# A trunk step on one core: a gate's product behind two lower halves, three norm sums one unit on, and two window sums behind the last split of an activation sum

## The chip, the cores and the metric

The kernel runs on one core of a Trainium2 chip. A core has a matrix engine (PE, with its weight loads shown as PEld), three elementwise engines (DVE, ACT, POOL) and a queue that issues most transfers (SP). The metric is the device time of one execution in microseconds (us), the median over the runs; lower is better.

## The reference

One inference step of a two-layer trunk on 1024 prompt tokens and 8 x 8 sample tokens, 1088 columns in all, all in float32. Layer 0 is a Mamba-2 (SSD) mixer, layer 1 a pooling mixer, each behind a modulated norm; a last norm follows. Cut to what this case touches:

```python
# layer 0, per group g of 8 (256 channels each)
y, new_ssm = ssd_scan(xs, dt, A, Bm, Cm, ssm_prev)
y = (y + d_skip[:, None] * xs).reshape(b, L, D_INNER)
gated = (y * silu(z)).reshape(b, L, N_GROUPS, D_INNER // N_GROUPS)
gated = gated * rsqrt(mean(gated * gated, -1) + EPS)          # one norm per group
out = (gated.reshape(b, L, D_INNER) * norm_g) @ w_out
# layer 1
uz = h @ w_in;  u, z = uz[..., :2048], uz[..., 2048:]
for g, w in enumerate((2, 4, 8, 16)):                          # 512 channels each
    win_sum = cs[off:off+L] - cs[off-w:off-w+L]                # sum over the last w rows of u
    groups.append(win_sum / cnt - u[g])
mixed = einsum(groups, w_group) * ch_scale * silu(z)
out = mixed @ w_out
```

## The kernel before

Activations lie with channels on the 128 partitions and the 1088 tokens along the row. Every float32 operand of a large product is split into an upper half `hi` (an ACT copy to the short type) and a lower half `lo` (on DVE: the value minus `hi`), and a product is three matmuls: hi by hi, hi by lo, lo by hi. A matmul chunk is 368, 368 and 352 columns (`CH`) in layer 0's direct products, and 272 columns in the products that save a multiplication by sums of blocks (tile name `st`).

The Python code writes instructions in program order, and the framework's scheduler then fixes one order for each engine; `self.tc.issue_after(ins)` around a call says that what is written inside is to be placed behind `ins` in that order. Each engine runs its own list strictly in turn, so an instruction that waits holds all that stand behind it. Semaphores make engines wait for one another.

Layer 0's scan is `scan_group(g, T)`, a generator for each of 8 groups. Its steps are small, so `ssd_layer` fills PE between them with units of other work from `self.fill` (`beside`): projections first, and from group 4's last steps on the units of the output product, `op_first` and then `op_unit` (one chunk, 12 matmuls on four pairs of halves). `FILL[g]` says how many units follow each scan step. When a group's steps are done, its tail goes on as `rest` in the loop of the next group: step `next(rest)` at `i == 0` runs the norm sum, and step `next(rest)` at `i == 3` scales the rows by it.

The tail of a group: `gate(q)` multiplies 128 channels of the rows by the gate (L748 on DVE, tile `xbc<-xbc,z`), and squares them (L749 on ACT). `zsum` adds the two squares (L791 on DVE). L763 on PE sums over the channels with a matrix of ones (tile `ms`); ACT takes logarithm and exponent; a row goes out to memory (L768 on SP, `rsd`) and comes back to all partitions (L771 on SP, `rs`). L775 on DVE scales the gated rows with it, and they are stored for the output product (L778).

For group 4 the second gate is not made in the tail itself: it is kept as `gate_late` and called in `proj_group`, behind the evictions of the last projection, at the place where the output product begins. There `op_part_load` prepares four pairs of halves: a row tile `gr` comes in, ACT makes `gh` (L805), and DVE makes the lower half `gl` (L806). `op_first` multiplies first with all the upper halves (L830, L831), then with the lower ones (L835), and only then evicts its three chunks (L847 on DVE).

For groups 4, 5 and 6 the sum of the squares is put behind the eviction of a filling unit (`self.zsum(ins)` in `ssd_layer`); where the unit returns no eviction, it is made with L763.

Layer 1 begins with `pool_layer`: `plain_pairs` makes two plain tiles of u and z, and beside them `act_sums` forms sums and differences of activation blocks (L1001 on DVE) and splits them into halves with `split` (ACT L1004, DVE L1005), into new tiles `t` and into the blocks `hh`, `hl`. `fast_pairs` then runs products of 272 columns. Their weights come as sums too: `w_sums` adds weight blocks on POOL (L1042 and L1043, tile `sw`; L1047, L1049), and `split_half` splits each (ACT L182, DVE L184, tile `w`). After the first pair of products, `u_pool` is called for the two plain tiles as well (p = 0 and 1): it forms running sums over w rows by doubling (L929 on DVE: the first reads `u` at step 1, the later ones `ws`).

Of the kernel before, what the change touches and what calls it, by code (L numbers as in the profile page):

```python
# [8 lines left out]
F32 = mybir.dt.float32  # L9
F32R = mybir.dt.float32r  # L10
AF = mybir.ActivationFunctionType
ALU = mybir.AluOpType
# [17 lines left out]
PLAIN = 2  # L30
# [69 lines left out]
class Build:  # L100
# [296 lines left out]
    def proj_group(self, G):  # L397

        raws = []
        for ii in range(4):  # L400
            w = self.stream_next()
            raw = self.proj_begin(G, ii)
            raws.append(raw)
            if (G["g"], ii) == (BESIDE[-1], 3):
                self.proj_end(G, 2, raws[2], True)
                ps = [self.mm_tile() for _ in CH]
                for k in range(8):
                    for c, j in ((0, k), (1, k), (2, 0), (2, k)) if k == 1 else ((0, k), (1, k), (2, k))[:3 if k else 2]:
                        self.mm1(ps[c], w, j, self.hn[j], CH[c], j == 0, j == 7)
                    for j in (0, 1) if k == 1 else (k,) if k else ():  # L410
                        self.slots.free(*self.hn[j])
                    if 0 < k < 4:
                        next(self.prep)
                    elif k in ():
                        self.load_x(0, k - 0)
                    if k < 7:
                        yield
                for c in range(3):
                    ins = self.proj_evict(G, ii, raw, ps[c], c, False)
                with self.tc.issue_after(ins.ins):  # L420
                    for _ in range(2):
                        next(self.prep)
                    with self.tc.issue_after(self.op_hi):
                        self.gate_late()
                yield
                self.late = lambda: self.proj_end(G, ii, raw, True)
                return
            ada = self.ada_do(self.ada_plan[G["g"], ii]) if (G["g"], ii) in self.ada_plan else iter(())
            for c in range(3):
                ps = self.mm_tile()  # L430
                self.mm3(ps, w, self.hn, CH[c])
                self.proj_evict(G, ii, raw, ps, c, (G["g"], ii) != (BESIDE[-1], 2))
                if c != (0, 0, 2, 0)[ii]:
                    next(ada, None)
                yield
# [366 lines left out]
    def op_split(self, raw, part):  # L802
        hi, lo = self.slots.get("gh", F32R, short=True), self.slots.get("gl", F32R, short=True)
        with self.tc.issue_after(self.front_copy) if 0 < part < 3 else contextlib.nullcontext():
            self.op_hi = self.nc.scalar.activation(hi, raw, AF.Copy).ins  # L805
        self.nc.vector.tensor_tensor(out=lo, in0=raw, in1=hi.bitcast(F32), op=ALU.subtract)  # L806
        self.slots.free(raw)
        return hi, lo

# [107 lines left out]
    def u_pool(self, p, U):  # L917

        nc, gi, (raw, rv) = self.nc, p // 4, U
        w = WINDOWS[gi]  # L920
        npl = self.gp2.tile([P, 9, 15], F32, tag="npl", bufs=2, name=self.name("npl"))
        nc.gpsimd.tensor_copy(npl[:, 0:1, :], raw[:, 1024:1039].unsqueeze(1))
        nc.gpsimd.tensor_copy(npl[:, 1:9, :], rv[:, :, 8:23])
        nc.sync.dma_start(self.io["npT"][p], npl)
        s, step, m = raw, 1, WIDE
        while step < w:
            d = self.slots.get("ws", wide=True)
            m -= step
            nc.vector.tensor_tensor(out=d[:, :m], in0=s[:, :m], in1=s[:, step:step + m], op=ALU.add)  # L929
            if step > 1:  # L930
                self.slots.free(s)
            s, step = d, 2 * step
        o = 16 - w
        nc.vector.tensor_tensor(out=s[:, o:o + w - 1], in0=s[:, o:o + w - 1], in1=self.kc[:, K_CNT + 15 * gi:K_CNT + 15 * gi + w - 1], op=ALU.mult)
        pl = self.slots.get("pl")
        nc.vector.scalar_tensor_tensor(out=pl[:, :NP], in0=s[:, o:o + NP], scalar=1.0 / w, in1=raw[:, 15:1039], op0=ALU.mult, op1=ALU.subtract)
        sv = s[:, 1039:1223].rearrange("p (b w) -> p b w", w=23)[:, :, o:o + 8]
        nc.vector.scalar_tensor_tensor(out=pl[:, NP:TOK].rearrange("p (b i) -> p b i", i=8), in0=sv, scalar=1.0 / w, in1=rv[:, :, 15:23],
                                       op0=ALU.mult, op1=ALU.subtract)
        self.slots.free(raw, s)  # L940
        nc.sync.dma_start(self.pld[p], pl)
        self.slots.free(pl)
# [50 lines left out]
    def act_sums(self):  # L993


        nc, sl, x = self.nc, self.slots, self.x
        h1, h2 = slice(0, HALF), slice(HALF, TOK)
        self.T = {}

        def sub(out, x, y):  # L1000
            nc.vector.tensor_tensor(out=out, in0=x, in1=y, op=ALU.subtract)  # L1001

        def split(x, hi, lo):
            nc.scalar.activation(hi, x, AF.Copy)  # L1004
            nc.vector.tensor_tensor(out=lo, in0=x, in1=hi.bitcast(F32), op=ALU.subtract)  # L1005

        def new(i, k, x):
            t = sl.get("t", F32R)
            self.T[i, k] = t
            split(x, t[:, h1], t[:, h2])  # L1010

        t1 = []
        for k in range(4):
            p, r = x[k], x[k + 4]
            t1.append(x[k - 1][:, h2] if k % 2 else p[:, h1])
            sub(t1[k], p[:, h2], p[:, h1])
            sub(p[:, h2], r[:, h2], p[:, h2])
            sub(r[:, h2], r[:, h2], t1[k])
            sub(r[:, h1], r[:, h1], r[:, h2])
            new(2, k, r[:, h2])  # L1020
            new(3, k, p[:, h2])
            yield
            new(4, k, r[:, h1])
            sl.free(r)
            if k % 2:
                sl.free(p)
            yield
        for k in range(4):
            p, q = self.hn[k]
            split(t1[k], p[:, h2], q[:, h2])  # L1030
        sl.free(x[0], x[2])
# [554 lines left out]
    def ssd_layer(self):  # L1586
        nc, sl = self.nc, self.slots
# [6 lines left out]
        for g in range(8):  # L1594
            sc = self.scan_group(g, T[g])
            for i, n in enumerate(FILL[g]):
                next(sc)
                for j in range(n):
                    ins = next(self.fill)
                    if ins:  # L1600
                        self.zsum(ins)
                    if i == 0 and j == 0:
                        next(rest, None)
                    elif i == 3 and j == 0:
                        with self.tc.issue_after(self.hins), self.tc.issue_after(ins.ins) if ins else contextlib.nullcontext():
                            next(rest, None)
# [350 lines left out]
```

## Time and profile before

| what | value |
|---|---|
| median of 3 runs | 1591.47 us (1590.93 to 1593.26) |
| profiled execution | 1587.95 us |
| its span, first to last instruction | 1586.1 us |
| mean granted clock of the matrix engine | 0.997 |
| PE / PEld busy | 1569.5 us (99%) / 1506.7 us (95%) |
| DVE / ACT / POOL busy | 1299.7 / 790.7 / 536.9 us |

Busy time is the time with at least one instruction of the engine under way. In a timeline a row gives start, length, engine, line, operation, tiles (out<-in), shape and count; in square brackets stands the idle time of the engine before it and what ended it. Consecutive matmuls overlap, so their pace is read from start to start. A row of the waits gives the waiting instruction, what it waited for, the total in us, how many times, and the longest. A row of the stretches gives the busy time of each engine (with counts), then the granted clock of PE, the share of the transfer engines' time and GB/s.

### The profile page before, as it was taken

How to read it: one execution, taken by the hardware profiler on the slowest of the kernel's cores; microseconds unless marked ns; L12 is line 12 of the kernel's file. 1: busy time of each engine (PE TensorE's matmuls, PEld its weight loads, DVE VectorE, ACT ScalarE, POOL GpSimd, SP SyncE). 2: the span in 40 equal slices, each digit the busy share in tenths (PEclk: the TensorE clock that was granted, in tenths of full speed). 3: DMA queues.
4: the chain of work that ended last, by engine and by line, in shares of the span. 5: the costliest groups of instructions: out<-in, count | busy, mean ns of one | idle time of the engine just before them, and what ended most of it. 6: DMA issues, size and time to landing. Idle time of an engine off the chain costs nothing.

```text
span 1586.1 us, 30716 instructions
## 1 busy us (share of the span) xinstructions
PE 1569.5 (99%) x11946; PEld 1506.7 (95%) x11946; DVE 1299.7 (82%) x2152; ACT 790.7 (50%) x1512; POOL 536.9 (34%) x558
## 2 busy tenths in 40 slices
PE   9999999999999999999999999999999999999997
PEld 7899999999999899989999999999999999999997
DVE  6974789888899889889888858998889777667886
ACT  6663344466766666665455437533332233233364
POOL 0133556522332414121211232776566630000241
PEclk9999999999999999999999999999999999999999
DMA  9422232355555555678999532233333379565783
GB/s 356 168 101 96 84 113 81 111 190 174 165 172 174 164 201 162 217 255 294 325 335 313 173 124 73 70 136 101 117 114 117 102 250 366 138 178 176 163 175 124
DMA packets 122304, 275.57 MB, mean 174 GB/s; under 512 B 18192, under 2 KB 59312, under 8 KB 122160
## 3 DMA queue, kind: packets, MB, share of 16 engines
q1 hardware_dynamic: 117840, 259.79, 48.0%
q0 software_dynamic: 4032, 12.72, 4.6%
q8 instruction: 94, 1.54, 0.4%
q10 hardware_dynamic: 288, 1.11, 0.2%
q14 instruction: 50, 0.41, 0.1%
HBM read 201.12 MB, written 70.23 MB: 171 GB/s over the span
## 4 chain that ended last, share of the span: by engine, by line
PE 88%; DVE 6%; ACT 2%; POOL 2%; issue 1%; DMA 1%; DVEq 0%; ACTq 0%; POOLq 0%
PE st L1079 11%; PE st L1077 11%; PE st L1078 11%; PE mm L190 11%; PE mm L191 11%; PE mm L192 10%; PE op L1297 2%; PE op L1298 2%; PE op L1296 2%; PE y L645 2%; PE S L623 2%; PE y L649 1%; PE tr L584 1%; PE am L261 1%; POOL sw L1042 1%; PE tr L581 1%
## 5 line engine op out<-in xcount | busy, mean ns | idle before, releaser
L1079 PE MATMUL st<-hh,w 128*128 128x272 f32 x832 | 240.6, 289 | 0.0
L1077 PE MATMUL st<-hh,w 128*128 128x272 f32 x832 | 240.4, 289 | 0.0
L1078 PE MATMUL st<-hl,w 128*128 128x272 f32 x832 | 240.4, 289 | 0.0
L1079 PE MATMUL st<-t,w 128*128 128x272 f32 x624 | 179.9, 288 | 0.6 <-DVE w L184 0.6
L1077 PE MATMUL st<-t,w 128*128 128x272 f32 x624 | 180.0, 288 | 0.0
L1078 PE MATMUL st<-t,w 128*128 128x272 f32 x624 | 179.5, 288 | 0.0
L190 PE MATMUL mm<-hh,wh 128*128 128x368 f32 (+1 forms) x528 | 179.2, 339 | 0.0
L191 PE MATMUL mm<-hl,wh 128*128 128x368 f32 (+1 forms) x528 | 174.3, 330 | 0.0
L192 PE MATMUL mm<-hh,wl 128*128 128x368 f32 (+1 forms) x528 | 173.4, 328 | 0.0
L1077 PEld LDWEIGHTS st<-hh,w 128*128 128x128 f32 x832 | 157.0, 189 | 0.0
L1078 PEld LDWEIGHTS st<-hl,w 128*128 128x128 f32 x832 | 157.0, 189 | 0.0
L1079 PEld LDWEIGHTS st<-hh,w 128*128 128x128 f32 x832 | 156.7, 188 | 0.0
L182 ACT ACTIVATE w<-wr 128x512 fp32r<-128x512 f32 x104 | 65.0, 629 | 165.7 <-PE st L1079 134.1
L631 POOL TENSOR_TENSOR hd<-h,cd 128x256 f32<-128x256 f32 x56 | 46.1, 824 | 291.4 <-DVE h L632 126.6
L1296 PE MATMUL op<-b,w 128*128 128x272 f32 x448 | 129.6, 289 | 0.0
L1297 PE MATMUL op<-b,w 128*128 128x272 f32 x448 | 129.0, 288 | 0.2 <-DVE b L1225 0.2
L1298 PE MATMUL op<-b,w 128*128 128x272 f32 x448 | 129.1, 288 | 0.0
L190 PE MATMUL mm<-gh,wh 128*128 128x368 f32 (+1 forms) x372 | 125.3, 338 | 0.0
L192 PE MATMUL mm<-gh,wl 128*128 128x368 f32 (+1 forms) x372 | 122.5, 329 | 0.0
L191 PE MATMUL mm<-gl,wh 128*128 128x368 f32 (+1 forms) x372 | 122.3, 329 | 0.2 <-DVE gl L806 0.2
L1079 PEld LDWEIGHTS st<-t,w 128*128 128x128 f32 x624 | 117.5, 188 | 0.8 <-DVE w L184 0.8
L1077 PEld LDWEIGHTS st<-t,w 128*128 128x128 f32 x624 | 117.8, 189 | 0.4 <-ACT w L182 0.3
(310 smaller groups left out, 4613.3 us busy)
## 6 DMA issues: line engine op xcount, KB each, us to landing
wr<-win SPq DMA_DIRECT2D x48, 512.0 KB, 3.7
wr<-pin SPq DMA_DIRECT2D x32, 512.0 KB, 3.8
acb<-acd SPq DMA_DIRECT2D x60, 256.0 KB, 4.7
wr<-pout SPq DMA_DIRECT2D x28, 512.0 KB, 5.4
x<-x1d SPq DMA_DIRECT2D x24, 544.0 KB, 6.1
x1d<-x SPq DMA_DIRECT2D x22, 544.0 KB, 4.3
wr<-pout POOLq DMA_DIRECT2D x20, 512.0 KB, 5.6
x<-xT SPq DMA_DIRECT2D x16, 544.0 KB, 6.9
```

Source lines behind the costliest of these rows:

```text
L182: self.last_hi = self.nc.scalar.activation(hi, src, AF.Copy)
L190: nc.tensor.matmul(ps[:, :n], hi[:, k, :], ah[:, a:a + n], start=first, stop=False)
L191: nc.tensor.matmul(ps[:, :n], hi[:, k, :], al[:, a:a + n], start=False, stop=False)
L192: nc.tensor.matmul(ps[:, :n], lo[:, k, :], ah[:, a:a + n], start=False, stop=last)
L623: nc.tensor.matmul(S[:, 256 * i:256 * i + 256], Bt, xde.rearrange("p r q -> p (r q)"), start=True, stop=True)
L631: nc.gpsimd.tensor_tensor(out=hd, in0=h[-1], in1=cd.unsqueeze(2).to_broadcast([P, 4, 64]), op=ALU.mult)
L1077: nc.tensor.matmul(ps[c][:, :QUART], hi[:, k], xh[:, t], start=(k == 0), stop=False)
L1078: nc.tensor.matmul(ps[c][:, :QUART], hi[:, k], xl[:, t], start=False, stop=False)
L1079: nc.tensor.matmul(ps[c][:, :QUART], lo[:, k], xh[:, t], start=False, stop=(k == 3))
L1296: nc.tensor.matmul(ps[:, :QUART], hi[:, k], xh, start=k == 0, stop=False)
L1297: nc.tensor.matmul(ps[:, :QUART], hi[:, k], xl, start=False, stop=False)
L1298: nc.tensor.matmul(ps[:, :QUART], lo[:, k], xh, start=False, stop=k == 7)
```

## The change

```diff
@@ proj_group
                     for _ in range(2):
                         next(self.prep)
-                    with self.tc.issue_after(self.op_hi):
+                    with self.tc.issue_after(self.op_hi), self.tc.issue_after(self.op_lo):
                         self.gate_late()
@@ op_split
-        self.nc.vector.tensor_tensor(out=lo, in0=raw, in1=hi.bitcast(F32), op=ALU.subtract)
+        self.op_lo = self.nc.vector.tensor_tensor(out=lo, in0=raw, in1=hi.bitcast(F32), op=ALU.subtract).ins
@@ u_pool
-            nc.vector.tensor_tensor(out=d[:, :m], in0=s[:, :m], in1=s[:, step:step + m], op=ALU.add)
+            with self.tc.issue_after(self.t_last) if p < PLAIN and step == 1 else contextlib.nullcontext():
+                nc.vector.tensor_tensor(out=d[:, :m], in0=s[:, :m], in1=s[:, step:step + m], op=ALU.add)
@@ act_sums.split
-            nc.vector.tensor_tensor(out=lo, in0=x, in1=hi.bitcast(F32), op=ALU.subtract)
+            self.t_last = nc.vector.tensor_tensor(out=lo, in0=x, in1=hi.bitcast(F32), op=ALU.subtract).ins
@@ ssd_layer
                     if ins:
                         self.zsum(ins)
-                    if i == 0 and j == 0:
+                    if i == 0 and j == (g > 4):
                         next(rest, None)
```

It has three parts, and the instructions themselves stay the same in number and shape. (1) Group 4's late gate is placed behind the two lower halves that the output product's first unit needs. (2) For the tails of groups 4, 5 and 6 the step with L763 is written one filling unit later. (3) The first window sum of the two plain tiles is placed behind the last split of `act_sums`.

Part 1 on DVE, where the output product begins. Before (`gl` are lower halves, `ea`, `cb`, `xd` and `M` belong to the scan, `wl` is a weight's lower half):

```order
L748 TENSOR_TENSOR xbc_7600<-xbc_7600,z_8232 128x1088
L610 TENSOR_TENSOR ea_8654<-xbc_8367,ea_8654 128x512
L610 TENSOR_TENSOR ea_8737<-xbc_8367,ea_8737 128x512
L145 TENSOR_TENSOR wl_8501<-wr_8327,wh_8500 128x1024
L806 TENSOR_TENSOR gl_8485<-gr_8416,gh_8484 128x1088
L806 TENSOR_TENSOR gl_8489<-gr_8482,gh_8488 128x1088
L595 TENSOR_TENSOR cb_8540<-tr_8527,kc 128x128
L600 TENSOR_TENSOR xd_8543<-tr_8527,tkx_1450 128x512
L598 TENSOR_TENSOR M_8534<-M_8534,cb_8540 128x512
L791 TENSOR_TENSOR z_8230<-z_8230,z_8232 128x1088
L847 SCALAR_TENSOR_TENSOR x_8494<-mm_8506,gat_278,x_8494 128x368
```

The same place on DVE now:

```order
L610 TENSOR_TENSOR ea_8654<-xbc_8367,ea_8654 128x512
L610 TENSOR_TENSOR ea_8737<-xbc_8367,ea_8737 128x512
L145 TENSOR_TENSOR wl_8501<-wr_8327,wh_8500 128x1024
L806 TENSOR_TENSOR gl_8485<-gr_8416,gh_8484 128x1088
L806 TENSOR_TENSOR gl_8489<-gr_8482,gh_8488 128x1088
L748 TENSOR_TENSOR xbc_7600<-xbc_7600,z_8232 128x1088
L595 TENSOR_TENSOR cb_8540<-tr_8527,kc 128x128
L600 TENSOR_TENSOR xd_8543<-tr_8527,tkx_1450 128x512
L598 TENSOR_TENSOR M_8534<-M_8534,cb_8540 128x512
L847 SCALAR_TENSOR_TENSOR x_8494<-mm_8506,gat_278,x_8494 128x368
L847 SCALAR_TENSOR_TENSOR x_8494<-mm_8507,gat_278,x_8494 128x368
```

The gate's product L748 has moved behind the two L806, and the sum L791 behind the three evictions L847.

Part 2 on PE, at the tail of group 6 (inside group 7's loop). Before, L763 stands inside the second filling unit (`mm_10330`):

```order
L192 MATMUL mm_10305<-gh_10196,wl_10066 128x368
L190 MATMUL mm_10330<-gh_9850,wh_10065 128x352
L763 MATMUL ms_10319<-z_10016,ones 32x272 x4
L191 MATMUL mm_10330<-gl_9851,wh_10065 128x352
L192 MATMUL mm_10330<-gh_9850,wl_10066 128x352
```

Now it stands behind that whole unit (`mm_10319` here):

```order
L190 MATMUL mm_10319<-gh_10196,wh_10065 128x352
L191 MATMUL mm_10319<-gl_10197,wh_10065 128x352
L192 MATMUL mm_10319<-gh_10196,wl_10066 128x352
L763 MATMUL ms_10336<-z_10016,ones 32x272 x4
L581 MATMUL tr_10351<-xbc_10156,xbc_10155 128x128
```

It moved by 11 matmuls; at the tail of group 5 it moves by 12 in the same way. At the tail of group 4 it moves by 18, and three transposes of the scan (L584) that stood behind it, some two units on, now stand ahead of both units. On SP, L768 and L771 of these tails move with it. For group 4 a store and a row tile that stood between the two now stand ahead of both; a modulation weight and a second row tile, which stood behind L771, stand ahead of it; and an `x` tile that stood right behind L771 stands behind one more store and two loads of `acb`.

Part 3 on DVE, at the end of `act_sums` (`x`, `t`, `hl` are its sums and splits, `w` a weight's lower half). Before:

```order
L1001 TENSOR_TENSOR x_10372<-x_10908,x_10372 128x544
L929 TENSOR_TENSOR ws_12404<-u_11751 128x1222
L1001 TENSOR_TENSOR x_10908<-x_10908,x_10259 128x544
L184 TENSOR_TENSOR w_12155<-wr_11765,w_12155 128x512
L1005 TENSOR_TENSOR t_12059<-x_10668,t_12059 128x544
L1001 TENSOR_TENSOR x_10908<-x_10908 128x544
L929 TENSOR_TENSOR ws_12406<-ws_12404 128x1220
L1005 TENSOR_TENSOR t_12092<-x_10837,t_12092 128x544
L1005 TENSOR_TENSOR t_12138<-x_10908,t_12138 128x544
L1005 TENSOR_TENSOR hl_11497<-x_10255,hh_11496 128x544
```

Now (all lines behind L929 count one more, since the change adds a line there):

```order
L1006 TENSOR_TENSOR hl_11501<-x_10259,hh_11500 128x544
L1006 TENSOR_TENSOR hl_11503<-x_10259,hh_11502 128x544
L930 TENSOR_TENSOR ws_12404<-u_11751 128x1222
L184 TENSOR_TENSOR w_12158<-sw_12149,w_12158 128x512
L184 TENSOR_TENSOR w_12169<-wr_12029,w_12169 128x512
L930 TENSOR_TENSOR ws_12406<-ws_12404 128x1220
L935 TENSOR_TENSOR ws_12406<-ws_12406,kc 128x3
```

Both sums of the first plain tile have left the chain of splits: the first stands right behind it, the second behind two splits of weights. POOL's list is the same before and after.

## The prediction

> **What bounds the kernel.** I began with the page. PE is busy for 99% of the span, and the chain that ended last runs on PE for 88% of it; so only time in which PE stands, or runs slowly, can be won.
>
> ```profile
> span 1586.1 us, 30716 instructions
> PE 1569.5 (99%) x11946; PEld 1506.7 (95%) x11946; DVE 1299.7 (82%) x2152; ACT 790.7 (50%) x1512; POOL 536.9 (34%) x558
> ```
>
> Then the waits of PE: three of its rows name instructions that the change touches, the lower halves (L806), the sum of squares (L791) and a weight's lower half (L184). They are 2.3 + 0.7 + 0.6 = 3.6 us.
>
> ```profile
> PE mm L835 <- DVE gl L806: 2.3, 2, 1.6
> PE ms L763 <- DVE z L791: 0.7, 2, 0.4
> PE st L1079 <- DVE w L184: 0.6, 1, 0.6
> ```
>
> Third, the timelines of PE and DVE around the longest of them.
>
> ```profile
> 706.57 0.33 PE L830 MATMUL mm<-gh,wh 128*128 128x368 f32 x1
> 706.74 0.33 PE L831 MATMUL mm<-gh,wl 128*128 128x368 f32 x1
> 706.90 0.32 PE L830 MATMUL mm<-gh,wh 128*128 128x352 f32 x1
> 707.06 0.32 PE L831 MATMUL mm<-gh,wl 128*128 128x352 f32 x1
> 707.22 0.50 PE L835 MATMUL mm<-gl,wh 128*128 128x368 f32 x2
> 709.30 0.44 PE L835 MATMUL mm<-gl,wh 128*128 128x368 f32 x1 [1.58 <-DVE gl L806]
> 710.51 3.03 PE L835 MATMUL mm<-gl,wh 128*128 128x368 f32 x9 [0.76 <-DVE gl L806]
> 713.37 0.39 PE L581 MATMUL tr<-xbc,xbc 128*128 128x128 f32 x2
> ...
> 704.43 1.28 DVE L748 TENSOR_TENSOR xbc<-xbc,z 128x1088 f32<-128x1088 f32 x1
> 705.63 1.28 DVE L610 TENSOR_TENSOR ea<-xbc,ea 128x512 f32<-128x512 f32 x2
> 707.97 2.48 DVE L806 TENSOR_TENSOR gl<-gr,gh 128x1088 fp32r<-128x1088 f32 x2
> 710.57 0.68 DVE L600 TENSOR_TENSOR xd<-tr,tkx 128x512 f32<-128x512 f32 x1
> 711.77 1.28 DVE L791 TENSOR_TENSOR z<-z,z 128x1088 f32<-128x1088 f32 x1
> 712.97 1.52 DVE L847 SCALAR_TENSOR_TENSOR x<-mm,gat,x 128x368 f32<-128x368 f32 x3
> ```
>
> PE runs out of upper halves at 707.2 and waits twice, once for each L806. Something more is in these rows: the matmuls ahead of the wait start 0.17 us (368 columns) and 0.16 us (352 columns) apart, but the nine behind it take from 710.51 to 713.37, 0.32 us each. The stretches say why: the granted clock is 0.51 there.
>
> ```profile
> 706.50:709.90 3.40, 1.66 (x9) 1.10 (x7) 3.40 (x4) 1.94 (x3) 0.00 (x0) 1.00 0.95 375
> 709.90:713.30 3.40, 2.79 (x9) 2.80 (x10) 3.40 (x6) 0.00 (x0) 0.00 (x0) 0.51 0.84 261
> ...
> 20.40:23.90 3.50, 2.56 (x28) 2.23 (x20) 2.49 (x12) 2.51 (x6) 0.00 (x0) 1.00 1.03 416
> ```
>
> After a stretch of 3.4 us with 1.74 us of idle PE the clock halves for 3.4 us; a stretch with 0.94 us idle (20.40) was not followed by a drop.
>
> The Trainium skill ("TensorE: Matmul & The Clock Gate", section "HAM oscillation — how this bites in real kernels") warns of idle gaps over some 3.4 us. By that rule waits of 2.3 us would cost no clock, and term 1b below would be nothing; here the trace shows a drop behind 2.3 us, and the measurement decides.
>
> **Part 1, the late gate.** L748 starts at 704.43 and the next row at 705.63: it takes 1.20 us of DVE ahead of both L806. Behind them it gives each a start 1.20 us earlier; the ACT copies that they need were ready, as DVE never stood. The first wait falls from 1.58 to 0.38, the second stays at 0.76, being L806's own length behind the first. **1a: 1.20 us.** Bounds 0 and 1.58.
>
> 1b, the clock. Five matmuls at 0.17 us and four at 0.16 make 1.49 us where the rows show 2.86: 1.37 us lost. The waits that remain sum to 1.14 us in any 3.4 us stretch. That lies between 0.94 (no drop) and 1.74 (drop), much nearer the first, so I take the drop as gone. **1b: 1.37 us.** Bounds 0 (it drops still) and 1.7, half of a fully used stretch.
>
> Against that stands that DVE isn't earlier behind the three: L748 only changes places. L600, which PE's next scan product needs, still ends at 711.25, and the first L847, which frees the tile of the second unit, can begin at 711.77, where L791 stood, and end at about 712.4. PE at full speed is through the nine at 709.3 + 1.5 = 710.8, and with some 1.5 us of transposes and scan products at that unit at about 712.3. **New waits: 0.25 us lost** (0 to 0.6, one L847). The three transposes that now stand earlier cost the same where they stand; their tile was read last by L600, too. L749 on ACT follows L748 and comes some 4 us later than before (L748 moves from 704.4 to 709.2, ending 710.4); L791, behind three L847, needs it at 713.7 only.
>
> **Part 2, the norm sums.** At groups 5 and 6 PE waited in front of L763:
>
> ```profile
> 782.52 0.67 PE L763 MATMUL ms<-z,ones 128*32 128x272 f32 x8 [0.29 <-DVE z L791]
> ...
> 850.17 0.67 PE L763 MATMUL ms<-z,ones 128*32 128x272 f32 x8 [0.40 <-DVE z L791]
> ```
>
> L763 goes behind 12 and 11 more matmuls, about 1.9 us of PE work, and L791 is no later: both waits end. **0.69 us** (bounds 0 and 0.69). At group 4 there was no wait to remove; there L763 lands near 715.4 and L791 ends near 715.0. What comes later is the chain behind: ACT's logarithm, L768 and L771 on SP, L775 on DVE.
>
> ```profile
> 719.29 0.74 SPq L771 DMA_DIRECT2D rs<-rsd  x1
> 730.51 1.34 DVE L775 SCALAR_TENSOR_TENSOR xbc<-xbc,vec,rs 128x1088 f32<-128x1088 f32 x1
> ...
> rs<-rsd SPq DMA_DIRECT2D x8, 544.0 KB, 6.3
> ```
>
> L771 lands at the median at 719.3 + 6.3 = 725.6, 4.9 us ahead of L775. Now L763 is 0.7 us later, a weight's issue more stands ahead (0.4), and L775 comes up to 2.3 us earlier with PE: 1.5 us are left. The tails of groups 5 and 6 lose 1.6 to 1.9 us of similar slack. The SP rows that changed places (`x`, `acb`, `gr`, a weight) are issued within some 10 us of each other; the `x` tile that goes back is for a unit more than 10 us on. I cost them at nothing; the units between are the cover.
>
> **Part 3, the window sums.** PE waits at 1021.72 for a lower half whose origin is on POOL:
>
> ```profile
> 997.75 20.76 POOL L1042 TENSOR_TENSOR sw<-wr 128x512 f32<-128x512 f32 x1 [7.55 <-PE pl L191]
> ...
> 1028.49 1.69 POOL L1042 TENSOR_TENSOR sw<-wr 128x512 f32<-128x512 f32 x1 [4.84 <-DMA wr<-pin]
> ...
> 1007.64 1.41 DVE L929 TENSOR_TENSOR ws<-u 128x1222 f32<-128x1222 f32 x1
> 1011.49 1.41 DVE L929 TENSOR_TENSOR ws<-ws 128x1220 f32<-128x1220 f32 x1
> 1015.37 1.98 DVE L1005 TENSOR_TENSOR hl<-x,hh 128x544 fp32r<-128x544 f32 x3
> 1020.57 1.10 DVE L184 TENSOR_TENSOR w<-sw,w 128x512 fp32r<-128x512 f32 x1 [3.22 <-ACT w L182]
> ...
> 1020.25 0.29 PE L1079 MATMUL st<-hh,w 128*128 128x272 f32 x1
> 1021.72 0.39 PE L1079 MATMUL st<-t,w 128*128 128x272 f32 x1 [0.61 <-DVE w L184]
> 1021.95 0.29 PE L1077 MATMUL st<-t,w 128*128 128x272 f32 x1
> ```
>
> The same L1042 takes 1.69 us elsewhere and 20.76 here: it ends 1.2 us after DVE's unbroken row of two-input operations ends at 1017.35. The two L929 are 2.7 us of that row. Now the second is out of it, and the first still follows without a break, so POOL comes free 1.35 us earlier, or more if DVE, now ahead of ACT's copies, stands for a moment. L184 then ends at 1021.67 - 1.35 = 1020.3, when PE arrives. From 1020.25 to 1021.95 PE makes four starts that take 0.125 us each elsewhere: 1.2 us lost. **I take 1.1 us** (0 if POOL gains nothing, 1.2). The second sum now stands in front of a later L184; DVE began that stretch 1.35 us earlier, which pays for it.
>
> The Trainium skill ("SBUF — State Buffer", section "SBUF: two separate sides") says that DVE and GpSimd share a port pair as a lock, held for one whole instruction by whichever starts first. Read so, POOL would have got its turn between two DVE operations, the sums would not matter, and the total below would be 3.0 us instead of 4.1; the 20.76 us row speaks against that.
>
> **The sum.** 1.20 + 1.37 - 0.25 + 0.69 + 1.10 = 4.1 us. The profiled execution took 1587.95 us, 3.5 below the median of the runs, so it would become 1583.8; from the median, 1591.47 - 4.1 = **1587.4 us**, 0.26% less. A measurement here tells about 0.2% (3.2 us) from no change.
>
> **Rivals.** (A) The clock stays out of it: it drops still in the new kernel, since 1.14 us is above the only stretch known to be harmless, or it did not drop in most timed runs of before. For it: one profile is one execution. Against: the bound lies nearer the harmless one. Then 4.1 - 1.4 = 2.7 us remain: 1588.8, no measurable change. The Trainium skill (same page, section "What's actually happening") calls the observing window free-running, so that a wait may fall into one window or across two from run to run; no run here shows it.
> (B) Part 3 does nothing, POOL being freed no earlier because the first sum still follows the splits at once. Against: the second sum does leave. 4.1 - 1.1 = 3.0 us: 1588.5.
> (C) Slower, by a wait in place of those removed: `rs` of group 4 lands late and DVE stands at L775 with the scan's updates and evictions behind it. PE can run on for two or three tiles, some 4 us. To end slower by 0.2% PE must lose 4.1 + 3.2 = 7.3 us, so `rs` must land 1.5 + 4 + 7.3 = 12.8 us later than reckoned, 19 us after its issue instead of 6.3. Then 1594.7 or more. No median of a transfer there speaks for it.
>
> **How the numbers follow.** Forecast 0.60, its own range 1586.2 to 1588.8; A 0.22; B 0.09; C 0.05; other small new waits that eat the gain 0.04. The line of 0.2% is at 1588.3. Of the forecast some 0.50 lies below it, of A 0.04, of B 0.02: faster 0.56. Slower 0.06, same 0.38. The range 1585.8 (all upper bounds: 1.58 + 1.7 + 0.69 + 1.2 = 5.2, and 0.5 for the spread of the runs) to 1590.4 (A and B at once leave 1.6, less 0.5 of new waits) leaves out C and little else.
>
> **What would show it.** Right: L835 waits about 0.4 and 0.8 us; no stretch behind it under a clock of 1.00; no wait in front of L763; L1042 ends near 1014 (1018.5, less 1.35 and the 3.0 us that parts 1 and 2 bring before it), and PE doesn't wait for L184. Wrong: a granted clock of 0.5 behind L835; L1079 still waiting; new waits of PE for L847 or L600 near 712, or DVE standing at L775.

## The result, and the profile after

| | median (lowest to highest), runs | ratio to the kernel before, 95% interval |
|---|---|---|
| before, beside the changed kernel | 1590.66 us (1588.43 to 1593.26), 12 | |
| changed | 1586.93 us (1585.85 to 1589.05), 12 | 0.9977 [0.9969, 0.9986] |

The change brought 3.7 us, 0.23%, between 2.2 and 4.9 us by the interval. The forecast was 1587.4 us, 4.1 us less than before, its range 1585.8 to 1590.4. The size is right. Of the gains that were added up, part 3's 1.10 us did not come, and the gain of part 2 was read from an execution in which PE waited little.

The profiled execution took 1586.18 us. First the page, and the rows of the waits that touch the change:

```profile
span 1584.0 us, 30719 instructions
PE 1568.2 (99%) x11946; PEld 1504.7 (95%) x11946; DVE 1302.7 (82%) x2152; ACT 790.8 (50%) x1512; POOL 528.4 (33%) x558
...
PE mm L835 <- DVE gl L806: 1.1, 2, 0.8
...
PE st L1080 <- DVE w L184: 0.5, 1, 0.5
...
PE st L1079 <- DVE t L1006: 0.4, 1, 0.4
```

The wait for L806 has halved and the one of L763 is gone. The wait for L184 is still there (L1080 now; lines behind L929 count one more), and a new one, for a lower half t of L1006, stands beside it.

The place of part 1 on PE's timeline:

```profile
707.23 0.50 PE L835 MATMUL mm<-gl,wh 128*128 128x368 f32 x2
708.10 0.43 PE L835 MATMUL mm<-gl,wh 128*128 128x368 f32 x1 [0.37 <-DVE gl L806]
709.30 1.76 PE L835 MATMUL mm<-gl,wh 128*128 128x368 f32 x9 [0.77 <-DVE gl L806]
710.89 0.38 PE L581 MATMUL tr<-xbc,xbc 128*128 128x128 f32 x2
```

The stretches there, cut at the limits found below:

```profile
708.07:711.49 3.42, 2.62 (x16) 2.38 (x17) 3.42 (x5) 1.01 (x1) 0.00 (x0) 1.00 0.89 299
711.49:714.90 3.41, 3.41 (x24) 3.32 (x23) 3.41 (x9) 0.66 (x3) 0.00 (x0) 1.00 0.94 321
```

The waits are 0.37 and 0.77 us, and the nine matmuls behind them take 1.59 us from the first start to the L581, against 2.86 before: the granted clock is 1.00 throughout.

The place of part 3 on POOL's timeline:

```profile
994.99 11.09 POOL L1043 TENSOR_TENSOR sw<-wr 128x512 f32<-128x512 f32 x1 [7.57 <-PE pl L191]
1006.15 1.65 POOL L1044 TENSOR_TENSOR sw<-sw,wr 128x512 f32<-128x512 f32 x1
```

On DVE's:

```profile
1004.21 2.45 DVE L1002 TENSOR_TENSOR x<-x,x 128x544 f32<-128x544 f32 x2
1006.58 1.77 DVE L184 TENSOR_TENSOR w<-wr,w 128x512 fp32r<-128x512 f32 x1
1008.27 1.82 DVE L1002 TENSOR_TENSOR x<-x 128x544 f32<-128x544 f32 x1
...
1016.42 1.43 DVE L930 TENSOR_TENSOR ws<-u 128x1222 f32<-128x1222 f32 x1
1017.76 0.69 DVE L184 TENSOR_TENSOR w<-sw,w 128x512 fp32r<-128x512 f32 x1
...
1020.43 1.13 DVE L935 TENSOR_TENSOR ws<-ws,kc 128x3 f32<-128x3 f32 x1
1022.43 0.71 DVE L1006 TENSOR_TENSOR t<-x,t 128x544 fp32r<-128x544 f32 x1
```

And on PE's:

```profile
1018.51 0.39 PE L1080 MATMUL st<-t,w 128*128 128x272 f32 x1 [0.50 <-DVE w L184]
1023.20 0.39 PE L1079 MATMUL st<-t,w 128*128 128x272 f32 x1 [0.42 <-DVE t L1006]
```

POOL's operation, 20.76 us before, takes 11.09 and ends at 1006.1, far earlier than forecast. But from there on DVE's operations of 0.7 us take 1.7 to 1.8 while POOL's next two run, so DVE gives back what POOL won. The first sum then stands in front of L184 (1016.42), the second and L935 in front of a t that PE waits for (1020.43).

How far the same PE instruction starts ahead of its time in the profile of before gives the account: 0.00 us from 571 to 709, 1.21 at the second waiting L835, 2.48 behind the clock stretch (713), 2.38 at 721, 2.04 at 737, 2.34 behind group 5's tail (792), 2.81 behind group 6's (918), 2.77 at 1000, 2.64 at 1026, 2.10 at the end.

### The profile page after: what moved, and what is told of

Its sections match the earlier page's. It is cut to its first block, busy times and chain, and to the rows that moved or that the text cites. A ratio compares the mean times of both kernels' runs of the same rounds, so it can differ in the third digit from the quotient of the medians.

```text
span 1584.0 us, 30719 instructions
## 1 busy us (share of the span) xinstructions
PE 1568.2 (99%) x11946; PEld 1504.7 (95%) x11946; DVE 1302.7 (82%) x2152; ACT 790.8 (50%) x1512; POOL 528.4 (33%) x558
## 4 chain that ended last, share of the span: by engine, by line
PE 89%; DVE 5%; issue 3%; DMA 2%; ACT 1%; POOL 0%; SPq 0%; DVEq 0%; ACTq 0%; POOLq 0%
PE st L1079 11%; PE st L1080 11%; PE st L1078 11%; PE mm L190 11%; PE mm L191 11%; PE mm L192 11%; PE op L1298 3%; PE op L1299 3%; PE op L1297 3%; PE y L645 2%; PE S L623 2%; PE y L649 2%; PE tr L584 1%; PE am L261 1%; PE tr L581 1%
## 5 line engine op out<-in xcount | busy, mean ns | idle before, releaser
L1080 PE MATMUL st<-hh,w 128*128 128x272 f32 x832 | 240.2, 289 | 0.0
L1080 PE MATMUL st<-t,w 128*128 128x272 f32 x624 | 179.6, 288 | 0.5 <-DVE w L184 0.5
L1080 PEld LDWEIGHTS st<-hh,w 128*128 128x128 f32 x832 | 156.4, 188 | 0.0
L1080 PEld LDWEIGHTS st<-t,w 128*128 128x128 f32 x624 | 117.3, 188 | 0.7 <-DVE w L184 0.7
```

Of the source, the lines that this page charges most:

```text
L1080: nc.tensor.matmul(ps[c][:, :QUART], lo[:, k], xh[:, t], start=False, stop=(k == 3))
```

## The experiments

Kernels with the same value under "before there" share their runs of the kernel before. The ratio is estimated from all the runs and is not the quotient of the two medians beside it. A kernel with one run has a profile and no interval.

| kernel | median us, runs | before there | ratio [95%] |
|---|---|---|---|
| changed, again | 1586.64, 12 | 1590.43 | 0.9981 [0.9973, 0.9989] |
| parts 1 and 2 | 1586.62, 11 | 1590.43 | 0.9980 [0.9970, 0.9989] |
| same, second sum late | 1584.13, 5 | 1590.43 | 0.9966 [0.9953, 0.9979] |
| same, both sums late | 1586.39, 10 | 1590.43 | 0.9977 [0.9968, 0.9986] |
| part 1 | 1591.00, 10 | 1589.77 | 1.0002 [0.9992, 1.0012] |
| part 2 | 1588.01, 10 | 1589.77 | 0.9990 [0.9980, 0.9999] |
| part 3 | 1590.07, 10 | 1589.77 | 1.0007 [0.9998, 1.0017] |
| part 2, PE kept busy | 1590.34, 1 | 1589.77 | |
| parts 1 and 2, group 4's tail alone | 1586.66, 11 | 1589.49 | 0.9987 [0.9978, 0.9997] |
| second sum late, again | 1585.74, 10 | 1589.49 | 0.9978 [0.9968, 0.9987] |
| changed, short filler on DVE | 1585.07, 1 | 1589.49 | |
| before, again | 1589.72, 1 | 1589.49 | |

### Part 3: length of the row, or its first break?

The first question was why part 3 brought nothing. Two theories: the row of DVE operations is what counts, by its length (the prediction's); or POOL gets in at the first break in the row. By the single records, neighbouring operations in that row overlap by some 0.07 us, but of the two L1002 at 1004.21 the second begins 0.03 us after the first has ended: it needs the first's output, and the sum that stood between them has left. POOL's L1043 ends 1.14 us later. In before, it ended 1.16 us behind the row's end.

The changed kernel, unedited:

> The changed kernel once more, beside the others on one chip. Break theory (POOL takes the port in the first 0.03 us break between two dependent DVE subtractions, which the first window sum used to fill; what PE then waits for stands behind a window sum on DVE): POOL's first L1043 ends near 1006 again, about 11 us after its start, and PE waits about 0.5 us for L184 and 0.4 us for the split L1006. Rival, the profile of the change was a chance: the long POOL operation ends near 1014 to 1016 in this profile, and the two waits are not there. Time against before: 0.9975 to 0.9985 by both.

It measured 0.9981; POOL took 11.09 us again, PE waited 0.49 and 0.41 us again.

Parts 1 and 2 alone:

```diff
-            with self.tc.issue_after(self.t_last) if p < PLAIN and step == 1 else contextlib.nullcontext():
-                nc.vector.tensor_tensor(out=d[:, :m], in0=s[:, :m], in1=s[:, step:step + m], op=ALU.add)
+            nc.vector.tensor_tensor(out=d[:, :m], in0=s[:, :m], in1=s[:, step:step + m], op=ALU.add)
...
-            self.t_last = nc.vector.tensor_tensor(out=lo, in0=x, in1=hi.bitcast(F32), op=ALU.subtract).ins
+            nc.vector.tensor_tensor(out=lo, in0=x, in1=hi.bitcast(F32), op=ALU.subtract)
```

> Parts 1 and 2 of the change without part 3: the window sums stand where they stood before. Break theory: POOL's L1042 takes about 20 us and ends when DVE's row of splits ends, PE waits 0.6 us for L184 and for no split; time within 0.5 us of the changed kernel, ratio to before near 0.9978. Length theory (the prediction's: part 3 brings 1.1 us): this kernel is 1.1 us slower than the changed one, ratio near 0.9985. The clock of PE does not drop behind L835 by either.

It measured 0.9980, the same as the whole change. A gain of 1.1 us (0.0007) from part 3 would still lie inside the two intervals, so the trace has to say it, and it does: PE's lead falls by 0.13 us over part 3's place in the changed kernel, against the 1.1 forecast.

The first sum where it was, and the second behind T[3,3]'s lower half (in `u_pool`, and in `act_sums.new`):

```diff
-            with self.tc.issue_after(self.t_last) if p < PLAIN and step == 1 else contextlib.nullcontext():
+            with self.tc.issue_after(self.t33) if p < PLAIN and step == 2 else contextlib.nullcontext():
...
             split(x, t[:, h1], t[:, h2])
+            if (i, k) == (3, 3):
+                self.t33 = self.t_last
```

> Parts 1 and 2; the first window sum stays between the two dependent subtractions, and only the second one goes, far back, behind the last split of the third activation sum. Break theory: with the break filled POOL stays out past 1006 as in before; DVE's row of splits is 1.35 us shorter, nothing stands in front of L184, so PE's wait for L184 (1.2 us by starts) goes and no new one comes: 1.0 us faster than parts 1 and 2 alone, ratio near 0.9972. Rival, the second sum was what opened the row for POOL: L1043 ends near 1006 here too. Rival, part 3 can bring nothing: the same time as parts 1 and 2 alone.

Both sums behind T[3,3] (with the same lines in `act_sums.new`):

```diff
-            with self.tc.issue_after(self.t_last) if p < PLAIN and step == 1 else contextlib.nullcontext():
+            with self.tc.issue_after(self.t33) if p < PLAIN and step == 1 else contextlib.nullcontext():
```

> Parts 1 and 2; both window sums go far back, behind the last split of the third activation sum. Break theory: POOL gets in near 1002 to 1003 and is done near 1006, its three operations and DVE's hold each other up so that the splits end about 2 us later than they would, but no sum stands in front of L184 or of the split: PE waits for neither, 1.0 to 1.2 us faster than the changed kernel, ratio near 0.9971. Rival, the hold-up between POOL and DVE alone makes PE wait: a wait of 0.4 us or more for L184 or L1006 stays and the time is that of the changed kernel.

POOL's operation in parts 1 and 2 alone:

```profile
995.03 20.74 POOL L1042 TENSOR_TENSOR sw<-wr 128x512 f32<-128x512 f32 x1 [7.57 <-PE pl L191]
```

With both sums late:

```profile
994.45 11.11 POOL L1045 TENSOR_TENSOR sw<-wr 128x512 f32<-128x512 f32 x1 [7.55 <-PE pl L191]
```

With the second late (the repeat of this kernel, below):

```profile
996.53 14.97 POOL L1045 TENSOR_TENSOR sw<-wr 128x512 f32<-128x512 f32 x1 [7.55 <-PE pl L191]
```

And PE in the kernel with both sums late:

```profile
1048.30 0.39 PE L1082 MATMUL st<-t,w 128*128 128x272 f32 x1 [0.71 <-POOL w L184]
```

Without the first sum between the two dependent operations 11.1 us, wherever the sum goes; with it there, 15.0, up to a break of 0.09 us where DVE waits for ACT's copy; with both sums in, 20.7. With both sums late the waits for L184 and t are gone, but a new one of 0.71 us stands two pairs later, and the time is that of parts 1 and 2. With the second late, no wait is left there.

Part 3 alone, from the kernel before:

```diff
+            with self.tc.issue_after(self.t_last) if p < PLAIN and step == 1 else contextlib.nullcontext():
...
+            self.t_last = nc.vector.tensor_tensor(out=lo, in0=x, in1=hi.bitcast(F32), op=ALU.subtract).ins
```

> Part 3 alone (first window sum behind the last split). Theory formed from the trace of the changed kernel (POOL gets in at the first break in DVE's row): L1043 lasts about 11 us instead of 20.8, DVE's splits then end later, PE waits some 0.5 us for L184 and 0.4 us for L1006, and the time is as before, within 0.5 us. Theory of the prediction (the row only becomes shorter): L1043 lasts about 19 us, no wait for L184, time 1.1 us below before. Both expect the two L806 waits and the clock drop of before unchanged.

POOL's timeline:

```profile
1002.95 11.11 POOL L1043 TENSOR_TENSOR sw<-wr 128x512 f32<-128x512 f32 x1 [7.55 <-PE pl L191]
```

The waits of PE:

```profile
PE st L1080 <- DVE w L184: 0.5, 1, 0.5
PE st L1079 <- DVE t L1006: 0.4, 1, 0.4
```

1.0007 [0.9998, 1.0017]: no gain, and the 1.1 us of the prediction (0.9993) lie outside. The 11 us and both waits do not come from parts 1 and 2.

The break closed on purpose: in the changed kernel a short operation between the two dependent ones (`pk` is the first of them).

```diff
-            sub(p[:, h2], r[:, h2], p[:, h2])
+            pk = nc.vector.tensor_tensor(out=p[:, h2], in0=r[:, h2], in1=p[:, h2], op=ALU.subtract).ins
+            if k == 3:
+                brk = self.gp2.tile([P, 128], F32, tag="brk", bufs=1, name=self.name("brk"))
+                with self.tc.issue_after(pk):
+                    nc.vector.tensor_tensor(out=brk, in0=self.kc[:, :128], in1=self.kc[:, :128], op=ALU.add)
             sub(r[:, h2], r[:, h2], t1[k])
```

> The changed kernel with one short extra operation of two inputs on DVE (128 columns of a constant added to themselves, read by nobody) between the two dependent L1002 where DVE's row had its first break of 0.03 us. If that break let POOL in: the row has no break there now, L1043 runs on until the next one (DVE is ahead of ACT's copies three or four operations later), ends about 4 to 6 us later than 1.1 us behind the pair and lasts 14.5 to 17 us instead of 11.1; PE's wait for L184 goes or shrinks. If only the length of the row or a fixed time of POOL counted: 11 us again.

POOL's timeline:

```profile
995.37 13.81 POOL L1047 TENSOR_TENSOR sw<-wr 128x512 f32<-128x512 f32 x1 [7.57 <-PE pl L191]
```

DVE's:

```profile
1005.24 0.28 DVE L1022 TENSOR_TENSOR brk<-kc 128x128 f32<-128x128 f32 x1
...
1007.31 4.19 DVE L1006 TENSOR_TENSOR t<-x,t 128x544 fp32r<-128x544 f32 x3
```

A filler of 0.28 us made POOL's operation 2.7 us longer (13.81; the expectation had 14.5 to 17, so the next break came a little sooner than reckoned). That break is one of 0.09 us in front of the second of the three L1006, which is stretched like the operations behind the break of the changed kernel; POOL's operation ends 1.15 us behind the start of this break. PE's wait for L184 is gone; 0.3 us for t are left. So it is the first break that lets POOL in, not the length of the row. This filler had one execution, but all fourteen profiles agree: POOL's operation ends 1.14 to 1.16 us behind the end of the last DVE operation ahead of the first break, or ahead of the row's end.

### Parts 1 and 2, and the clock

Part 1 alone:

```diff
-                    with self.tc.issue_after(self.op_hi):
+                    with self.tc.issue_after(self.op_hi), self.tc.issue_after(self.op_lo):
...
-        self.nc.vector.tensor_tensor(out=lo, in0=raw, in1=hi.bitcast(F32), op=ALU.subtract)
+        self.op_lo = self.nc.vector.tensor_tensor(out=lo, in0=raw, in1=hi.bitcast(F32), op=ALU.subtract).ins
```

> Part 1 alone (L748 behind both L806). Theory of the prediction (1a 1.2 us of waits, 1b 1.4 us of clock): L835 waits 0.4 and 0.8 us, the nine matmuls behind them stay under 0.17 us from start to start at a granted clock of 1.00, the L763 waits of 0.3 and 0.4 us are still there; the time is 2.0 to 2.6 us below before. Rival, the clock drops in both or in neither of most executions: the waits shrink as said, but the time is only about 1.2 us below before.

The stretches, and then L763 on PE's timeline:

```profile
696.69:700.10 3.41, 2.42 (x14) 1.33 (x13) 3.41 (x6) 1.13 (x1) 0.00 (x0) 1.00 0.95 355
700.11:703.52 3.41, 3.41 (x14) 3.41 (x13) 3.41 (x4) 3.35 (x6) 0.00 (x0) 0.50 0.70 231
```
```profile
714.68 0.67 PE L763 MATMUL ms<-z,ones 128*32 128x272 f32 x8 [0.49 <-DVE z L791]
784.54 0.67 PE L763 MATMUL ms<-z,ones 128*32 128x272 f32 x8 [2.16 <-DVE z L791]
```

No gain: the interval excludes the 2.0 us of the prediction's theory and has the rival's 1.2 at its edge. The profile shows three candidates for the cause. The clock dropped 10 us earlier than in before, behind a wait of 0.99 us for an `xbc` of L615, and PE came so late to L835 that nothing was left to wait for. L763 of group 4, which never waited in before, waits 0.49 us: part 1 has put L791 behind three evictions. And L763 of group 5 waits 2.16 us where the profile of before had 0.29. The second follows from the edit; the first and third are this execution's, and what the other nine lost is not shown. Their clock was no better, though: the mean granted clock of the ten runs is 0.9974, and that of before beside them 0.9974.

Part 2 alone:

```diff
-                    if i == 0 and j == 0:
+                    if i == 0 and j == (g > 4):
```

> Part 2 alone (L763 one unit on). Theory: the waits in front of L763 go, the waits of 1.6 and 0.8 us for L806 stay, with a clock of 0.5 behind them; the time is 0.5 to 0.7 us below before. Rival, the later norm sums make something else late: a new wait in the three tails, time as before or above it.

PE's timeline, and the stretches:

```profile
709.60 0.43 PE L835 MATMUL mm<-gl,wh 128*128 128x368 f32 x1 [1.58 <-DVE gl L806]
710.80 1.75 PE L835 MATMUL mm<-gl,wh 128*128 128x368 f32 x9 [0.77 <-DVE gl L806]
712.39 0.38 PE L581 MATMUL tr<-xbc,xbc 128*128 128x128 f32 x2
```
```profile
705.71:709.12 3.41, 2.31 (x14) 1.96 (x13) 3.41 (x5) 3.03 (x4) 0.00 (x0) 1.00 1.02 396
709.12:712.53 3.41, 2.16 (x12) 1.92 (x13) 3.41 (x6) 0.00 (x0) 0.00 (x0) 1.00 0.92 318
```

The time fell by 1.6 us (0.2 to 3.2), against 0.5 to 0.7 expected; no L763 wait is left. And here both theories missed: the waits are those of before, 1.58 and 0.77 us, and yet the clock did not drop. The trace records each change of the granted clock, and all of them, in every profile, are whole multiples of 3.413 us after the first. In this execution a limit of these windows (709.12) cuts the first wait, and the two windows hold 1.10 and 1.25 us of idle.

The Trainium skill ("TensorE: Matmul & The Clock Gate", section "What's actually happening") says that activity is judged in a window of 3413 ns that runs freely, whatever the kernel does. These runs agree: the same two waits bring a drop in one execution and none in another. The rule of the same page (section "HAM oscillation — how this bites in real kernels") that gaps of more than some 3.4 us throttle is too lenient here: while PE had work, the drops stand behind windows with 0.99 to 2.34 us of idle.

To tell idle from anything else at this place, part 2 with extra matmuls in the two waits:

```diff
+                for _ in range({2: 7, 3: 4}.get(k, 0) if c == 0 else 0):
+                    nc.tensor.matmul(ps[2][:, 384:512], self.ones, self.ones, start=False, stop=False)
```

> Part 2 alone, with eleven extra 128-column matmuls on PE in the two waits for L806 (seven in front of the first waiting L835, four in front of the second); they write columns of a bank that nobody reads. DVE is as in part 2 alone. If the idle of PE is what halves the clock: the waits for L806 shrink by what the extra matmuls take (some 0.06 us each at full clock), the nine L835 and those behind them run at 0.17 us from start to start at a granted clock of 1.00. If the drop comes from something else at this place (the rush of the L835 themselves, or chance): the nine stay at 0.32 us and 0.5.

PE's timeline, and the stretch behind the waits:

```profile
707.95 0.49 PE L837 MATMUL mm<-gl,wh 128*128 128x368 f32 x2
708.28 1.72 PE L836 MATMUL mm<-ones 128*128 128x128 f32 x14
710.03 0.43 PE L837 MATMUL mm<-gl,wh 128*128 128x368 f32 x1
710.30 1.05 PE L836 MATMUL mm<-ones 128*128 128x128 f32 x8
711.23 1.75 PE L837 MATMUL mm<-gl,wh 128*128 128x368 f32 x9
```
```profile
711.48:714.89 3.41, 3.41 (x24) 3.41 (x24) 3.38 (x8) 0.28 (x1) 0.00 (x0) 1.00 0.85 288
```

(The profile counts each extra matmul twice; L837 is L835.) In this execution both waits lie in one window (708.06 to 711.47), as in before; filled, no drop follows. It is one execution, and it fits the idle of PE as what counts; part 2 without the extra matmuls had no drop either, but there the limit split the waits.

The kernel before, a second time:

> The kernel before, once more, for a second profile. If the clock drop behind L806 belongs to every execution: two waits of 1.6 and 0.8 us and a clock of 0.5 behind them again. If the place of the 3.41 us windows decides (as in the profile of part 2 alone, where the same two waits fell into two windows and no drop followed): waits as before, the drop only if one window holds both. The L763 wait near 785 is 0.3 us if the tile of ACT's L805 lands early, 1.8 us or more if it lands late.

The stretches, and L763 on PE's timeline:

```profile
708.22:711.63 3.41, 1.74 (x10) 1.19 (x9) 3.41 (x5) 1.06 (x1) 2.58 (x2) 1.00 0.80 296
711.64:715.05 3.41, 3.41 (x14) 3.17 (x12) 3.41 (x9) 0.28 (x1) 0.00 (x0) 0.50 0.81 268
```
```profile
784.53 0.67 PE L763 MATMUL ms<-z,ones 128*32 128x272 f32 x8 [1.80 <-DVE z L791]
```

The waits for L806 are 0.90 and 0.77 us here, for PE came later to the first; the window holds both, and the clock drops. The L763 wait is 1.80 us, not 0.29. What differs ahead of it is ACT's L805 of that group, behind which DVE's chain to L791 follows. In the first profile of before:

```profile
759.74 1.12 ACT L805 ACTIVATE gh<-gr 128x1088 fp32r<-128x1088 f32 x1 [4.98 <-DVE cb L597]
```

In this one:

```profile
761.75 1.11 ACT L805 ACTIVATE gh<-gr 128x1088 fp32r<-128x1088 f32 x1 [6.51 <-DMA x1d<-x]
```

In the next kernel:

```profile
757.08 1.11 ACT L805 ACTIVATE gh<-gr 128x1088 fp32r<-128x1088 f32 x1 [4.49 <-DMA x1d<-x]
```

In the second profile of before it starts 2.0 us later than in the first, and each step of DVE's chain from there to L791 is 2.0 us later, too, while PE arrives only 0.5 us later, which makes 0.29 + 1.5 = 1.8. The wait of ACT is put down to a transfer in two of the three, and its end moves from run to run.

Parts 1 and 2 without part 2 at groups 5 and 6:

```diff
-                    if i == 0 and j == (g > 4):
+                    if i == 0 and j == (g == 5):
```

> Part 1, and part 2 at the tail of group 4 alone (the tails of groups 5 and 6 as before). Theory formed from the profile of part 1 alone (part 1 sends L791 of group 4 behind three evictions, so that L763 waits 0.5 us there unless part 2 moves it): the L763 wait near 714 is gone, those of groups 5 (0.3 to 2.2 us, with a clock of 0.5 behind the long ones) and 6 (0.4 us) stay; the time lies between before and parts 1 and 2 together, at 1.0 to 2.5 us below before. Rival, the parts simply add up and the waits near 785 are worth no more than 0.7 us: 2.4 to 2.8 us below before, within 0.7 us of parts 1 and 2 together.

2.1 us less than before by the ratio (0.5 to 3.5; 2.8 by the two medians), so the theory and the rival cannot be told apart by the time. Group 4's wait is gone, as said; L835 waits 0.37 and 0.77 us in one window, with no drop behind. L805 came early here, and L763 of group 5 didn't wait at all (group 6: 0.40). So the figure says what part 2 does for part 1 at group 4; what groups 5 and 6 add on the median, about 1 us by the two ratios, is within their intervals.

The second sum late, a second time:

> Parts 1 and 2, the first window sum where it stood before and the second behind the lower half of T[3,3], a second time. If the second sum's place is what part 3 should have changed: no wait of PE for L184 and none for L1006, POOL's long operation about 15 us, and 0.6 us less than parts 1 and 2 alone, so some 3.5 to 5.5 us below before. If the lower time of the first runs (5 of them) was chance: about 3 us below before.

0.9978, where the first time gave 0.9966. In that first series the five runs lay some 2 to 2.5 us below parts 1 and 2 and below the changed kernel; beside other runs of before the repeat is level with both (0.9980, and 0.9977 and 0.9981). Which of the two is nearer the truth stays open. No wait for L184 or t, but another wait is large in both profiles of this kernel, here 1.9 us. The waits of PE, and of DVE between 715 and 737:

```profile
PE y L649 <- DVE h L632: 1.9, 1, 1.9
```
```profile
DVE xbc L775 <- DMA rs<-rsd: 2.2, 1, 2.2
```

The second is in the changed kernel, too:

```profile
DVE xbc L775 <- DMA rs<-rsd: 0.5, 1, 0.5
```

DVE stands at L775 for the `rs` of group 4's tail, with L632 behind it, on which PE's L649 waits. L771, which loads `rs` back once L768 has stored it, was issued at 719.29 in before. In the changed kernel, and in this one, on SP's queue:

```profile
721.30 0.38 SPq L771 DMA_DIRECT2D rs<-rsd  x1
```
```profile
723.46 0.32 SPq L771 DMA_DIRECT2D rs<-rsd  x1
```

In eight profiles DVE waits at L775 for 1.5, 0.5, 1.1, 0.6, 1.9, 2.2, 0.5 and 0.3 us (part 2 with PE kept busy, changed twice, parts 1 and 2, second sum late twice, both late, filler on DVE), and PE at L649 for 0.3 to 0.4 us less each time. The six others, part 2 alone and group 4's tail alone among them, show neither wait.

Apart from that open gain of the second sum late, no version here is faster than the changed kernel beyond the intervals.

## Why the prediction was right, and where it was wrong

**1a, 1.20 us: right.** 1.21 measured, and the waits of 0.37 and 0.77 us as forecast.

**1b, 1.37 us: right in this profile, and for a narrower reason than given.** 1.27 measured. The stretch was treated as if it could lie anywhere; it lies on a fixed grid. While PE still had work, all five windows with 1.67 us of idle or more (before twice, part 1, and two in part 3) were followed by a drop. A window with 1.75 us at the kernel's end was not (1574.45 to 1577.86 in the kernel with group 4's tail alone, where PE's last matmul ends in the window), so the amount alone doesn't decide. Of windows with 0.99 to 1.48 us three were (0.99, 1.13, 1.14 us; the last two stand near 22 us, where the change moves nothing) and eleven weren't, among them the 1.14 us that the kernel with group 4's tail alone left in one window. The 1.14 us that part 1 leaves are thus not safe by their amount. In the profiled execution of the change they fell into two windows, with 0.34 and 0.80. Rival A's second half (before did not always drop) came true in one, that of part 2 alone, of the four profiles with both waits at L835 and without part 1 (before twice, part 2 alone, part 3 alone).

The mean granted clock of every run gives an estimate of how often. One step of 3.413 us at half clock takes 0.0011 off it (0.5 x 3.413 / 1586). The mean over the runs is 0.9974 to 0.9976 in the three series of before, 0.9985 and 0.9984 in the two of the change, and 0.9984 in parts 1 and 2: about one step less in each execution, at whatever place. But part 1 alone has 0.9974, no better than before, part 2 alone 0.9977, and part 1 with part 2 at group 4's tail 0.9985. The saved clock that 1b ascribed to part 1 was thus seen only together with part 2 at group 4; which step it is in the timed runs, and why part 1 alone doesn't save it, stays open.

**New waits, 0.25 us lost: wrong place, and too small.** None came at L847 or L600 near 712. Between 713 and 737 the lead fell by 0.44 us, most of it at L649, behind L775. The step that failed here is "1.5 us are left": L771 was reckoned 1.1 us later than before (0.7 + 0.4), and it was issued 2.0 us later in the profile of the change and 4.2 in that of the second sum late, so DVE stood. Most of the excess lies between L768 and L771: 1.6 us in before, 2.7 and 4.9 in those two. The change alone does not explain it, as part 1 alone, with that tail where it was, has 4.7. That is rival C's place and its mechanism, at a tenth of its size: the wait of PE at L649 is 0 to 1.9 us in the seven profiles with all of parts 1 and 2, 0.7 us on their mean. Another 0.54 us of the lead goes between 1026 and the end, in small steps that were not followed.

**Part 2, 0.69 us: right in this profile (0.30 + 0.47), probably too small for the median.** Part 2 alone measured 1.6 us, with 0.69 inside its interval of 0.2 to 3.2. The price was read from one execution, in which L805 came early. The wait near 785 is 0, 0.29, 1.79, 1.80 and 2.16 us in the five profiles that keep that tail as it was, with a clock drop behind two of them (the 1.80 us were cut by a window's limit, and none followed); of the nine with part 2 there one has 0.13 us and the others none. A wait of 1.8 us with a clock drop behind it, in the other runs, would also account for most of what the prediction could only note, that the profiled execution lay 3.5 us below the median of its kernel; for those runs it is not shown. "At group 4 there was no wait to remove" missed that part 1 makes one, which part 2 then removes: part 1 alone gains nothing measurable.

**Part 3, 1.10 us: wrong, and this is the step that failed.** "The first still follows without a break, so POOL comes free 1.35 us earlier, or more if DVE stands for a moment." The sum itself was what kept the row closed. Without it POOL's operation ended at 1006.1 where about 1014 was forecast, and the row behind it was stretched: three operations of 0.7 us took 5.3, and DVE's splits ended at 1016.5. "L184 then ends when PE arrives" fell with it: it stood behind the first sum. And "the second sum now stands in front of a later L184 ... which pays for it" left out the t of L1006 behind both, for which PE now waits 0.42 us. Over that place the lead fell by 0.13 us. Rival B's outcome came, 3.0 us for parts 1 and 2 by the prediction's own sum, by another mechanism: not that POOL was freed no earlier, but that it was freed too early.

The Trainium skill ("SBUF — State Buffer", section "SBUF: two separate sides") describes a lock that whoever starts first holds for one whole instruction. The stretched rows look like that, each engine's operation waiting out the other's. But in a closed row the next DVE operation always came first: POOL stood through more than a dozen of them, until a gap of 0.03 us.

So the forecast met the time in part by luck, with two errors that point opposite ways: 1.2 us too much for part 3, and too little for part 2 in every execution with a long wait near 785 (1.5 to 1.9 us more, and up to 1.7 of clock), which is three of the five profiles. How often the timed runs have such a wait is not on record.

## What to carry to other kernels

Before a wait is priced from one profile, look whether it hangs on a transfer. A second profile of the unchanged kernel showed 1.8 us where the first had 0.3. When an operation is taken out of a full DVE row, look at what it stood between: if its neighbours depend on each other, a break opens there, and a waiting POOL operation starts and slows both. A step that is moved behind work to give it slack takes that slack from whoever waits for its result: here the norm sums' `rs`, a store and a load later, where PE lost up to 1.9 us.

## What the runs showed of the hardware that was not expected

- The granted clock changed only on a grid of 3.413 us, and while PE had work it halved for exactly one step: 1.67 us or more of idle PE within one step halved it for the next (five of five), 0.94 us or less never did, and between them both were seen. At the kernel's end one window with 1.75 us of idle did not halve it.
- A POOL operation that takes 1.69 us elsewhere stood 11.1, 13.8, 15.0 or 20.7 us beside the same kind of DVE row, ending each time 1.14 to 1.16 us behind the last operation ahead of the point where the row first broke off, by 0.03 or 0.09 us, or ended.
